# A hybrid decoder step: GpSimd's arithmetic moved to VectorE, adaLN's scale in two halves, and the first tokens' norm applied behind the first products

## The chip, the cores and the metric

The kernel runs on one core of one Trainium2 chip. The metric is the device time of one execution in microseconds, as the median of several runs; the profile is of one further execution. The core's engines are TensorE (PE, with its weight loads PEld), VectorE (DVE), ScalarE (ACT), GpSimd (POOL) and SyncE (SP). Each has its own instruction queue and takes it in order; DMAs are issued from queues of SP, ACT and POOL.

## The reference

One inference step of a decoder layer over 1,024 new prompt tokens and 8 sequences of 4 sampled tokens (1,056 tokens, width 1,024). Only what the change touches is shown:

```python
mod = jax.nn.silu(c) @ w_ada + b_ada
sh1, sc1, g1, sh2, sc2, g2 = jnp.split(mod, 6, axis=-1)
h = _rmsnorm(x, rms1_g) * (1 + sc1[:, None, :]) + sh1[:, None, :]
z = h @ w_in + b_in            # q, k, v, forget, glu_a, glu_b, gate_a, gate_b
o = attend(q, k, v, logf)
y_a = o.reshape(B, L, ATT_WIDTH) @ w_pa
y_b = _depthwise_causal_conv(u_pad, dw_w, dw_b)      # u = glu_a * sigmoid(glu_b)
y_b = jax.nn.silu(_layernorm(y_b, ln_g, ln_b)) @ w_pb + b_pb
m = gate_a * y_a + gate_b * y_b
x = x + g1[:, None, :] * (m @ w_o)
```

A SwiGLU feed-forward part with the same kind of norm and modulation follows.

## The kernel before, in words

**Precision and products.** Activations and weights are split in a high part and a remainder (`wh`, `wl` for weights, `ah`, `al` for activations). A product is three matmuls per 128 rows of the inner dimension: `wh` by `ah` (L327), `wh` by `al` (L328), `wl` by `ah` (L329). ACT rounds a weight to `wh` (L315), and the engine that `split_w` is given subtracts to get `wl` (L318). A weight tile is 128x1024 (eight inner blocks) or, for the two output projections of the branches, 128x512.

**Tokens.** They come in three chunks, c0 and c1 of 384 tokens and c2 of 288 (256 of the prompt and the 32 sampled ones). Tiles hold features on partitions.

**Start.** `ada(i)` makes one sixth of the adaLN vector: eight loads `wa` of 512 KB, 32 matmuls against the conditioning vectors (L161), a copy by ACT (L165), two transposes (L170) and an addition (L173). `ada(1)` is the scale; with it `gains` makes `gP` (L180) and `gS` (L181). For c0 and c1 `rstd_x` sums squares and gives the reciprocal root, `normalise` (L283) multiplies it onto x in place, and `split_scaled` splits x·gP into `ah` (L291, ACT) and `al` (L292, DVE). The products of four weights with c0 and c1 (the Q and K columns of two pairs of heads) are taken from these while the shift, `ada(0)`, is still being loaded. They are copied to `early` tiles by ACT (L412). c2 is split with the shift already in (`modulate`, L249 to L273). When the shift is there, `split_shifted` splits c0 and c1 once more with the shift (L300 DVE, L301 ACT, L302 half on POOL, half on DVE), and the shift's own share of the early products is added as a bias, from two extra columns of c2.

**After the start.** The remaining Q and K pairs and V follow (to about 219 us). The stage from 219 to 428 us computes the convolution branch's inputs (`glu`), the depthwise convolution on DVE (120 instructions at L528, 128x1024 each), the gates and the decoding attention (`decode_group`, L692 to L748). Attention over the prompt takes 428 to 690 us, with the layer norm of the convolution (`conv_ln`, sums at L775 to L777 and L231 on POOL) and the other parts of `ada` between. From 690 to 795 us `branch` computes the two output projections, with an addition by POOL at L968 for the attention branch. From 795 us on the output product and the feed-forward part run, where POOL does no arithmetic.

**What sets the order.** A framework schedules the instructions of each engine ahead of time. `in_order` pins an instruction to program order among pinned ones, and `tc.high_priority()` moves a block ahead. Each engine then takes its list in order and waits at each entry for what it needs. Weights come through three raw buffers `wr` and two pairs `wh`, `wl`, so the split of one weight can begin when the product before the last has ended.

```python
def w_in_tile(i, eng=dve, q=sp):
    return split_ahead(w_in[i], KD, eng, q=q)
        wb = w_in_tile(12 + ct, pool, pool)
```

The second `pool` in such calls is the queue that the load of the weight is issued from.

Of the kernel before, what the change touches and what calls it, by code (L numbers as in the profile page):

```python
# [9 lines left out]
F32 = mybir.dt.float32  # L10
# [3 lines left out]
OP = mybir.AluOpType  # L14
# [72 lines left out]
def hybrid_step(ctx, tc, xT, cT, vec, bvf, con, stT, ptab, ptabr, kcT, vc, lfc, w_ada, w_in, w_vfa, w_vfb,  # L87
# [4 lines left out]
    def mkpool(**kw):  # L92
        return tc.alloc_tile_pool(reuse_waits="tile", **kw)
# [47 lines left out]

    def load_x(c):
        o, n = CH[c]
        t = x0.tile([P, KD, n], F32, name=f"x{c}")
        in_order(sp.dma_start(t, xT[:, KD * o:KD * (o + n)].rearrange("p (k n) -> p k n", k=KD)))
        xt.append(t)


    act.activation(cTt, cTt, AF.Silu)
    wap = mkpool(name="wap", bufs=1, side="right")  # L150

    def ada(i, pl, tag, bufs, psum):

        ps = psum()
        for k in range(KD):
            w = pl.tile([P, KD, P], F32, name="wa", tag=tag, bufs=bufs).rearrange("p a b -> p (a b)")
            d = sp.dma_start(w, w_ada[k * P:(k + 1) * P, i * 1024:(i + 1) * 1024])
            if i < 2:
# [4 lines left out]
        with tc.high_priority() if i < 2 else nullcontext():  # L163
            s = ev(wp, "gev", 4)
            d = act.copy(s[:, :256], ps[:, :256])  # L165
            if i == 1:
                in_order(d)
# [7 lines left out]
            if i == 1:  # L175
                gains(0, V_RMS1, 8)

    def gains(i, vcol, sc):
        g = V[:, vcol:vcol + KD]
        dve.scalar_tensor_tensor(gP[:, i, :], mod[:, sc:sc + KD, 0], 1.0, g, op0=OP.add, op1=OP.mult)  # L180
        dve.scalar_tensor_tensor(gS[:, i, :, :], mod[:, sc:sc + KD, 1:9], 1.0,  # L181
                                 g.unsqueeze(2).broadcast_to([P, KD, DB]), op0=OP.add, op1=OP.mult)
# [39 lines left out]

    def sumsq(tiles, n, eng=dve):
        s = sm.tile([P, 400], F32, name="ssum", tag="ssum", bufs=2)
        for i, t in enumerate(tiles):
            if i == 0:
                act.activation(s[:, :n], t, AF.Square)
            else:
                q = ev(sm, "sq", 2, (P, 400))
                act.activation(q[:, :n], t, AF.Square)  # L230
                eng.tensor_tensor(s[:, :n], s[:, :n], q[:, :n], OP.add)  # L231
        return s
# [61 lines left out]

    def split_shifted(c, eng):
        x = xt[c]
        ah, al = A[c] = act_tiles(c)
        for k in range(KD):
            t = ev(w0p, "mt", 3)
            dve.tensor_scalar(t, x[:, k, :], gP[:, 0, k:k + 1], mod[:, k, 0:1], OP.mult, OP.add)  # L300
            act.copy(ah[:, k, :], t)  # L301
            (eng if k % 2 else dve).tensor_tensor(al[:, k, :], t, ah[:, k, :].bitcast(F32), OP.subtract)  # L302
# [42 lines left out]


    w0p = mkpool(name="w0p", bufs=1)
    load_x(0)
    in_order(sp.dma_start(C[:, :C_MASK], con[:, :C_MASK]))
    in_order(sp.dma_start(V, vec))  # L350
# [11 lines left out]
    first_w(1, pool)  # L362
    first_w(2, pool, w0p, ("wh0", "wl0"))
    first_w(3, pool, w0p, ("wh0", "wl0"))
    normalise(1, rstd_x(1))
    split_scaled(1, dve)
    load_x(2)
    ada(0, wap, "wa", 5, ps_tr)
    wap.release()
# [125 lines left out]
    def glu(ct):  # L495
# [3 lines left out]
        sp.dma_start(us[:, :, 0:KL], stT[ct].rearrange("p (b i) -> p b i", b=DB))  # L499
        wb = w_in_tile(12 + ct, pool, pool)  # L500
        sg = []
        for c in range(3):
# [4 lines left out]
            sg.append(t)  # L507
        wa = w_in_tile(8 + ct, pool, pool)
        for c in range(3):
# [243 lines left out]
    glu(1)  # L753
    gate(15, pool, pool)
    glu(2)
    gate(14, pool, pool)
    gate(13, pool, pool)
    glu(3)
    for i in (12, 11, 10):
        gate(i, pool, pool)  # L760

# [5 lines left out]
    def conv_ln(c):  # L767
# [15 lines left out]
        pr = rstd(sumsq(xc, n, pool), n, CW)  # L783
        for ct in range(4):
# [189 lines left out]
    gate(7, pool, sp)  # L974
    ap.release()
# [433 lines left out]
```

## Time and profile before

| what | value |
| --- | --- |
| median of 3 runs | 1636.25 us (1630.43 to 1641.71) |
| profiled execution, own time | 1629.88 us |
| its span from first to last instruction | 1628.1 us |
| mean granted clock of TensorE | 0.992 of full speed |
| PE busy | 1564.1 us (96%) |
| DVE busy | 1048.5 us (64%) |
| ACT busy | 697.3 us (43%) |
| POOL busy | 178.2 us (11%), 147 instructions |

Own time and span differ by 1.8 us that lie around the span. In rows of groups and of the timeline, the first number is the start (timeline) or the line, `x8` counts instructions joined in a row, and what stands in brackets behind a row is the idle time ahead of it on its engine with what ended it. The clock is given as a share of 2.4 GHz, so that 0.5 is 1.2 GHz.

### The profile page before, as it was taken

To read this page: it belongs to the slowest core of one execution; us is meant where nothing else is said; L and a number is where in the kernel's file an instruction comes from. 1 tells how busy PE (TensorE), PEld (TensorE's weight loads), DVE (VectorE), ACT (ScalarE), POOL (GpSimd) and SP (SyncE) were. 2 spreads that over 40 slices of the span, in tenths; PEclk is the share of its full clock that TensorE was granted. 3 is DMA by queue.
4 is the path that set the end of the run, shared out by engine and by line. 5 is a ranking of instruction groups with operands and counts; after the bars stand their busy time and mean duration, and the time that the engine had idled before them with its cause. 6 is when DMAs were issued, how large, how long until landed. Compare 5 with 4: busy or idle time off the path is not lost.

```text
span 1628.1 us, 29682 instructions
## 1 busy us (share of the span) xinstructions
PE 1564.1 (96%) x11280; PEld 1475.9 (91%) x11280; DVE 1048.5 (64%) x2161; ACT 697.3 (43%) x1398; POOL 178.2 (11%) x147
## 2 busy tenths in 40 slices
PE   6999999999999989999999999999999999999997
PEld 4899978788977878999899989999999999999997
DVE  6942469999888867244559995555555596324644
ACT  4552112121376766434426663333333375224342
POOL 2121022342220101024200000000000000000000
PEclk9999999999999999999999999999999999999998
DMA  9195476777787774453554322222222257424552
GB/s 358 65 305 177 144 218 184 249 243 201 213 235 242 210 211 153 143 175 114 185 175 150 120 88 92 80 79 80 79 79 80 79 184 242 129 82 142 187 178 81
DMA packets 141424, 261.86 MB, mean 161 GB/s; under 512 B 24634, under 2 KB 81594, under 8 KB 140642
## 3 DMA queue, kind: packets, MB, share of 16 engines
q1 hardware_dynamic: 102802, 209.37, 41.0%
q10 hardware_dynamic: 36384, 43.01, 7.6%
q0 software_dynamic: 2096, 7.60, 1.5%
q8 instruction: 88, 1.44, 0.4%
q14 instruction: 54, 0.44, 0.1%
HBM read 206.44 MB, written 53.48 MB: 160 GB/s over the span
## 4 chain that ended last, share of the span: by engine, by line
PE 72%; DVE 12%; DMA 7%; ACT 3%; issue 3%; POOL 2%; SPq 1%; ACTq 0%; DVEq 0%; POOLq 0%
PE mm L1177 25%; PE mm L1278 16%; PE mm L329 7%; PE mm L328 7%; PE mm L327 7%; DVE acc L528 4%; DMA wa<-w_ada 2%; DMA gev<-gD 2%; POOL wl L318 1%; PE ptr L874 1%; PE mm L561 1%; PE mm L560 1%; PE mm L562 1%; DMA sq<-hD 1%; PE ppv L887 1%
## 5 line engine op out<-in xcount | busy, mean ns | idle before, releaser
L327 PE MATMUL mm<-ah,wh 128*128 128x384 f32 (+2 forms) x768 | 252.9, 330 | 8.8 <-ACT gev L384 4.0
L1278 PE MATMUL mm<-f,wo 128*128 128x352 f32 x1584 | 256.8, 323 | 0.0
L1278 PEld LDWEIGHTS mm<-f,wo 128*128 128x128 f32 x1584 | 254.8, 188 | 0.0
L329 PE MATMUL mm<-ah,wl 128*128 128x384 f32 (+2 forms) x768 | 251.5, 329 | 2.2 <-POOL wl L318 2.2
L328 PE MATMUL mm<-al,wh 128*128 128x384 f32 (+2 forms) x768 | 252.6, 329 | 0.0
L1177 PE MATMUL mm<-c,wc 128*128 128x264 f32 x1776 | 235.3, 285 | 1.5 <-ACT gev L1182 0.9
L1177 PE MATMUL mm<-b,wc 128*128 128x264 f32 x1680 | 228.1, 286 | 3.7 <-DVE wc L1135 1.5
L1177 PEld LDWEIGHTS mm<-c,wc 128*128 128x128 f32 x1776 | 224.1, 188 | 2.4 <-ACT gev L1182 1.3
L1177 PEld LDWEIGHTS mm<-b,wc 128*128 128x128 f32 x1680 | 214.7, 189 | 5.1 <-ACT wc L1134 2.0
L528 DVE SCALAR_TENSOR_TENSOR acc<-u,vec,acc 128x1024 f32<-128x1024 f32 x120 | 173.9, 1471 | 1.2
L327 PEld LDWEIGHTS mm<-ah,wh 128*128 128x128 f32 x768 | 145.9, 190 | 18.3 <-issue 5.9
L328 PEld LDWEIGHTS mm<-al,wh 128*128 128x128 f32 x768 | 146.3, 190 | 11.2 <-issue 10.4
L318 POOL TENSOR_TENSOR wl<-wr,wh 128x1024 fp32r<-128x1024 f32 (+1 forms) x44 | 111.8, 2545 | 396.0 <-ACT wh L315 340.9
L1229 DVE TENSOR_TENSOR wo<-wr,wo 128x512 fp32r<-128x512 f32 x108 | 69.7, 646 | 129.5 <-ACT wo L1228 128.9
L329 PEld LDWEIGHTS mm<-ah,wl 128*128 128x128 f32 x768 | 146.1, 190 | 6.3 <-POOL wl L318 3.1
L1134 ACT CAST wc<-wr 128x512 fp32r<-128x512 f32 x144 | 88.6, 621 | 141.4 <-PE mm L1177 132.4
L1228 ACT CAST wo<-wr 128x512 fp32r<-128x512 f32 x108 | 63.2, 585 | 150.6 <-PE mm L1278 143.3
L1135 DVE TENSOR_TENSOR wc<-wr,wc 128x512 fp32r<-128x512 f32 x144 | 98.5, 689 | 36.0 <-ACT wc L1134 35.0
L315 ACT CAST wh<-wr 128x1024 fp32r<-128x1024 f32 (+1 forms) x64 | 59.7, 939 | 93.1 <-PE mm L328 56.6
L192 POOL MEMSET rv<- 128x5 f32 x7 | 0.7, 103 | 746.2 <-DVE rt L210 746.2
L329 PE MATMUL mm<-b,wl 128*128 128x264 f32 x256 | 72.3, 286 | 2.2 <-DVE wl L318 2.2
L327 PE MATMUL mm<-b,wh 128*128 128x264 f32 x256 | 72.9, 285 | 1.3 <-ACT wh L315 1.3
(294 smaller groups left out, 2735.5 us busy)
## 6 DMA issues: line engine op xcount, KB each, us to landing
wr<-w_fi SPq DMA_DIRECT2D x52, 512.0 KB
wa<-w_ada SPq DMA_DIRECT2D x48, 512.0 KB
wr<-w_fo SPq DMA_DIRECT2D x36, 512.0 KB
kt<-kcT SPq DMA_DIRECT2D x64, 256.0 KB
vt<-vc SPq DMA_DIRECT2D x64, 256.0 KB
hD<-h ACTq DMA_DIRECT2D x44, 264.0 KB
wr<-w_in SPq DMA_DIRECT2D x18, 512.0 KB
wr<-w_o SPq DMA_DIRECT2D x16, 512.0 KB
```

What stands on the lines that cost most here:

```text
L315: d = act.copy(wh[:, r, :], raw[:, r, :])
L318: eng.tensor_tensor(wl[:, r, :], raw[:, r, :], wh[:, r, :].bitcast(F32), OP.subtract)
L327: pe.matmul(ps[:, :n], wh[:, k, :], xh, start=(k == 0), stop=False)
L328: pe.matmul(ps[:, :n], wh[:, k, :], xl, start=False, stop=False)
L329: pe.matmul(ps[:, :n], wl[:, k, :], xh, start=False, stop=(k == nk - 1))
L528: dve.scalar_tensor_tensor(a[:, :NP], u[:, j:j + NP], wv[:, j:j + 1], a[:, :NP], op0=OP.mult, op1=OP.add)
L1134: act.copy(w[:, 0, :n], raw)
L1135: dve.tensor_tensor(w[:, 1, :n], raw, w[:, 0, :n].bitcast(F32), OP.subtract)
L1177: pe.matmul(ps[:, :HS], w[i][:, r, k * P:(k + 1) * P], x[s][:, k, :], start=(new and k == 0 and j == 0), stop=(k == 3 and j == 2), skip_gr ...
L1228: act.copy(x[:, 0, :], raw)
L1229: dve.tensor_tensor(x[:, 1, :], raw, x[:, 0, :].bitcast(F32), OP.subtract)
L1278: pe.matmul(ps[e][:, :n], w[r][:, k * P:(k + 1) * P], f[x], start=(k0 + k + i == 0), stop=(k0 + k == HT - 1 and i == 2))
```

## The change

GpSimd's arithmetic goes to VectorE: all 44 subtractions `wl` that it did (30 of 128x1024, 14 of 128x512), the 28 additions at L968, the sums of `conv_ln`, and its eight subtractions in `split_shifted`. It keeps memsets, some small copies and the DMA issues. The scale is made by `ada_half`, four loads of 512 KB for each half of its columns, and x of c0 is loaded in two halves, so that the first products can be taken from inner blocks 0 to 3. `normalise` is gone: c0 and c1 are split as they come, and the reciprocal root, copied to a tile `rx` in SBUF, is multiplied onto the first products by DVE where ACT copied them. The second split of c0 and c1 is done by `modulate`. The first four weights are split in two halves each. The loads of the shift have four buffers where they had five.

```diff
-    def load_x(c):
+    def load_x(c, k0=0, k1=KD):
...
+    def ada_half(i, half, pl):
+
+        ps = ps_tr()
+        o = i * 1024 + half * 512
+        for k in range(0, KD, 2):
+            w = pl.tile([P, 2, 512], F32, name="wa", tag="wa", bufs=4)
+            in_order(sp.dma_start(w, w_ada[k * P:(k + 2) * P, o:o + 512].rearrange("(k p) n -> p k n", p=P)))
+            for j in range(2):
+                for g in range(4):
+                    pe.matmul(ps[32 * g:32 * g + 32, :P], cTt[:, k + j, :], w[:, j, g * P:(g + 1) * P],
+                              start=(k + j == 0), stop=(k + j == KD - 1))
...
+            dve.scalar_tensor_tensor(gP[:, 0, k], mod[:, r, 0], 1.0, g, op0=OP.add, op1=OP.mult)
...
     def rstd_x(c):
         n = CH[c][1]
-        return rstd(sumsq([xt[c][:, k, :] for k in range(KD)], n), n, D)
-
-    def normalise(c, pr):
-
-        for k in range(KD):
-            x = xt[c][:, k, :]
-            dve.tensor_tensor(x, x, pr[:, :CH[c][1]], OP.mult)
+        r = w0p.tile([P, n], F32, name=f"rx{c}")
+        act.copy(r, rstd(sumsq([xt[c][:, k, :] for k in range(KD)], n), n, D)[:, :n])
+        return r
...
-    def split_shifted(c, eng):
...
-        step = 8 if pinned else nk
+        step = 4 if pinned else nk
...
-    load_x(0)
     in_order(sp.dma_start(C[:, :C_MASK], con[:, :C_MASK]))
     in_order(sp.dma_start(V, vec))
-    pr = rstd_x(0)
-    ada(1, wap, "wa", 5, ps_tr)
-    normalise(0, pr)
...
-    first_w(0, pool)
+    ada_half(1, 0, wap)
+    first_w(0, dve)
+    load_x(0, 0, 4)
+    first_w(1, dve)
+    first_w(2, dve, w0p, ("wh0", "wl0"))
+    load_x(0, 4)
+    ada_half(1, 1, wap)
     split_scaled(0, dve)
+    first_w(3, dve, w0p, ("wh0", "wl0"))
     load_x(1)
...
-    normalise(1, rstd_x(1))
     split_scaled(1, dve)
+    norms = [rstd_x(0), rstd_x(1)]
+    gains(0, V_RMS1, 8)
     load_x(2)
-    ada(0, wap, "wa", 5, ps_tr)
+    ada(0, wap, "wa", 4, ps_tr)
...
-            act.copy(early[c, i], ps[:, :384])
+            dve.tensor_tensor(early[c, i], ps[:, :384], norms[c], OP.mult)
...
-        split_shifted(c, pool)
+        modulate(c, xt[c], norms[c], 0, 0, w0p, dve)
...
-        wb = w_in_tile(12 + ct, pool, pool)
+        wb = w_in_tile(12 + ct, dve, pool)
...
-        pool.tensor_tensor(s[:, :n], xc[0], xc[1], OP.add)
+        dve.tensor_tensor(s[:, :n], xc[0], xc[1], OP.add)
...
-            w = split_ahead(w_p[j], 4, pool)
+            w = split_ahead(w_p[j], 4)
...
-        (pool if j < KD - 1 else dve).tensor_tensor(zg, zg, X(j)[:, o:o + HS], OP.add)
+        dve.tensor_tensor(zg, zg, X(j)[:, o:o + HS], OP.add)
```

Lines of the changed kernel are numbered otherwise: the products L327, L328, L329 are L336, L337, L338 there, `wl` L318 is L327, the convolution L528 is L539, `al` of x·gP L292 is L310.

SP's queue at the start, from its first entry, in the kernel before (`x` with 3072 elements is a chunk of 384 tokens):

```order
L138 DMA cT<-cT 128x256
L145 DMA x_89<-xT 128x3072
L349 DMA con<-con 128x256
L350 DMA vec<-vec 128x248
L157 DMA wa<-w_ada 128x1024 x8
L309 DMA wr<-w_in 128x1024
L145 DMA x_232<-xT 128x3072
```

The same place in the changed kernel (1536 elements are a half of c0):

```order
L138 DMA cT<-cT 128x256
L363 DMA con<-con 128x256
L364 DMA vec<-vec 128x248
L159 DMA wa<-w_ada 128x2x512 x4
L318 DMA wr<-w_in 128x1024
L146 DMA x_146<-xT 128x1536
L318 DMA wr<-w_in 128x1024 x2
L146 DMA x_146<-xT 128x1536
L159 DMA wa<-w_ada 128x2x512 x4
L318 DMA wr<-w_in 128x1024
L146 DMA x_238<-xT 128x3072
```

x of c0 moved from ahead of the scale's eight loads to behind its first four, in two halves, with three weights around them.

PE's list at the start, in the changed kernel, from the end of the 36 first products with c0 (`pst<-con,ssum` sums the squares, `ptr<-con,gev` is the transpose of a half of the scale; before, all 32 matmuls of `ada` and both transposes stood ahead of the first product):

```order
L337 MATMUL mm<-al_213,wh 128x384
L338 MATMUL mm<-ah_212,wl 128x384
L162 MATMUL ptr<-wa,cT 32x128 x24
L220 MATMUL pst<-con,ssum 128x1 x3
L162 MATMUL ptr<-wa,cT 32x128 x8
L168 MATMUL ptr<-con,gev 128x128
L336 MATMUL mm<-ah_212,wh 128x384 x3
L337 MATMUL mm<-al_213,wh 128x384
L338 MATMUL mm<-ah_212,wl 128x384
```

The second half's 32 matmuls now stand between products with c0: 36 of the 96 ahead of them, 60 behind.

DVE's list in the stage of the convolution, at its third channel block, before (`acc` is the convolution, `dt` the decoding attention):

```order
L528 SCALAR_TENSOR_TENSOR acc<-u,vec,acc 128x1024 x2
L701 SCALAR_TENSOR_TENSOR dt<-ppv,cr,ct 128x4
L528 SCALAR_TENSOR_TENSOR acc<-u,vec,acc 128x1024 x13
L700 TENSOR_SCALAR dt<-pss,cr 128x512
L528 SCALAR_TENSOR_TENSOR acc<-u,vec,acc 128x1024 x2
```

And in the changed kernel:

```order
L539 SCALAR_TENSOR_TENSOR acc<-u,vec,acc 128x1024
L712 SCALAR_TENSOR_TENSOR dt<-ppv,cr,ct 128x4
L539 SCALAR_TENSOR_TENSOR acc<-u,vec,acc 128x1024 x9
L327 TENSOR_TENSOR wl<-wr,wh 128x1024
L539 SCALAR_TENSOR_TENSOR acc<-u,vec,acc 128x1024 x8
L711 TENSOR_SCALAR dt<-pss,cr 128x512
L539 SCALAR_TENSOR_TENSOR acc<-u,vec,acc 128x1024 x2
L711 TENSOR_SCALAR dt<-pss,cr 128x512
L327 TENSOR_TENSOR wl<-wr,wh 128x1024
L539 SCALAR_TENSOR_TENSOR acc<-u,vec,acc 128x1024 x2
```

A `wl` that had POOL's list to itself now stands behind up to nine steps of the convolution, and convolution steps stand behind it.

## Rows read from the trace of the kernel before

**Rows 1.** Page, part 1: busy time, share of the span and instructions of each engine.
```profile
PE 1564.1 (96%) x11280; PEld 1475.9 (91%) x11280; DVE 1048.5 (64%) x2161; ACT 697.3 (43%) x1398; POOL 178.2 (11%) x147
```

**Rows 2.** Busy time by stage: length, engines, then PEclk, DMA share, GB/s.
```profile
0.00:26.80 26.80, 12.03 (x78) 5.04 (x78) 11.69 (x35) 7.60 (x14) 2.55 (x5) 1.00 0.89 347
...
219.00:428.00 209.00, 202.81 (x1344) 169.03 (x1337) 206.46 (x225) 40.60 (x64) 60.90 (x24) 0.99 0.76 229
428.00:690.00 262.00, 248.65 (x1772) 216.65 (x1771) 183.36 (x576) 166.75 (x334) 34.36 (x29) 0.99 0.65 195
690.00:795.00 105.00, 101.08 (x716) 99.41 (x716) 49.80 (x92) 46.60 (x103) 43.32 (x43) 1.00 0.48 149
```

**Rows 3.** Timeline, 0 to 32.5 us: start, length, engine, line, operation.
```profile
10.64 2.28 PE L161 MATMUL ptr<-wa,cT 128*32 128x256 f32 x16 [10.64 <-DMA wa<-w_ada]
...
21.24 1.08 PE L161 MATMUL ptr<-wa,cT 128*32 128x256 f32 x8
21.34 3.81 DVE L283 TENSOR_TENSOR x<-x,pst 128x384 f32<-128x384 f32 x8 [2.66 <-PE pst L220]
...
26.86 0.69 PE L327 MATMUL mm<-ah,wh 128*128 128x384 f32 x1 [3.36 <-ACT ah L291]
...
28.32 0.52 PE L327 MATMUL mm<-ah,wh 128*128 128x384 f32 x1
...
28.64 0.52 PE L328 MATMUL mm<-al,wh 128*128 128x384 f32 x1
...
31.99 0.34 PE L327 MATMUL mm<-ah,wh 128*128 128x384 f32 x1
...
32.17 0.33 PE L328 MATMUL mm<-al,wh 128*128 128x384 f32 x1
```

**Rows 4.** Timeline of PE, then of DVE, 54 to 74 us.
```profile
55.54 0.97 PE L327 MATMUL mm<-ah,wh 128*128 128x384 f32 x4
...
73.75 0.44 PE L327 MATMUL mm<-ah,wh 128*128 128x290 f32 x2
...
61.09 0.21 DVE L173 TENSOR_TENSOR mod<-ptr,vec 128x72 f32<-128x72 f32 x1
...
69.69 0.42 DVE L269 TENSOR_TENSOR al<-ms,ah 128x256 fp32r<-128x256 f32 x1
```

**Rows 5.** Groups of POOL, then DVE by form: count, busy, mean ns, idle before.
```profile
L318 POOL TENSOR_TENSOR wl<-wr,wh 128x1024 fp32r<-128x1024 f32 (+1 forms) x44 | 111.8, 2545 | 396.0 <-ACT wh L315 340.9 <-PE mm L329 16.6 <-PE pss L818 15.1
...
L528 DVE SCALAR_TENSOR_TENSOR acc<-u,vec,acc 128x1024 f32<-128x1024 f32 x120 | 173.9, 1471 | 1.2
...
L318 DVE TENSOR_TENSOR wl<-wr,wh 128x1024 fp32r<-128x1024 f32 x20 | 24.4, 1231 | 6.8 <-ACT wh L315 6.6
...
L967 DVE TENSOR_TENSOR gev<-mm,gev 128x264 f32<-128x264 f32 x32 | 13.6, 426 | 15.5 <-ACT gev L956 13.7 <-PE mm L329 1.7
L283 DVE TENSOR_TENSOR x<-x,pst 128x384 f32<-128x384 f32 x16 | 7.6, 542 | 2.7 <-PE pst L220 2.7
```

**Rows 6.** Timeline of DVE and POOL, 320 to 428 us, and of PE at 339.
```profile
320.93 15.63 DVE L528 SCALAR_TENSOR_TENSOR acc<-u,vec,acc 128x1024 f32<-128x1024 f32 x13
399.55 28.47 DVE L528 SCALAR_TENSOR_TENSOR acc<-u,vec,acc 128x1024 f32<-128x1024 f32 x17
...
322.14 16.62 POOL L318 TENSOR_TENSOR wl<-wr,wh 128x1024 fp32r<-128x1024 f32 x1 [16.69 <-ACT wh L315]
...
400.14 2.96 POOL L318 TENSOR_TENSOR wl<-wr,wh 128x1024 fp32r<-128x1024 f32 x1 [11.27 <-ACT wh L315]
424.31 2.64 POOL L318 TENSOR_TENSOR wl<-wr,wh 128x1024 fp32r<-128x1024 f32 x1 [9.95 <-ACT wh L315]
...
338.81 0.57 PE L329 MATMUL mm<-ah,wl 128*128 128x384 f32 x1 [2.22 <-POOL wl L318]
```

**Rows 7.** What PE waited for, whole span: us in total, times, longest.
```profile
PE mm L329 <- POOL wl L318: 5.0, 5, 2.2
```

**Rows 8.** Busy time after that wait: PEclk is the third number from the end.
```profile
339.00:342.30 3.30, 3.30 (x11) 3.30 (x11) 3.27 (x2) 0.00 (x0) 3.01 (x3) 0.50 0.86 299
```

More of the change, by code (lines that the diff above doesn't have):

```diff
@@ L140, in hybrid_step @@
     in_order = tc.keep_in_program_order
-    def load_x(c):
+    def load_x(c, k0=0, k1=KD):
         o, n = CH[c]
-        t = x0.tile([P, KD, n], F32, name=f"x{c}")
-        in_order(sp.dma_start(t, xT[:, KD * o:KD * (o + n)].rearrange("p (k n) -> p k n", k=KD)))
-        xt.append(t)
+        if k0 == 0:
+            xt.append(x0.tile([P, KD, n], F32, name=f"x{c}"))
+        in_order(sp.dma_start(xt[c][:, k0:k1, :],
+                              xT[:, KD * o + k0 * n:KD * o + k1 * n].rearrange("p (k n) -> p k n", n=n)))
     act.activation(cTt, cTt, AF.Silu)
     wap = mkpool(name="wap", bufs=1, side="right")
+    def ada_half(i, half, pl):
[8 more added lines that the diff above has]
+                              start=(k + j == 0), stop=(k + j == KD - 1))
+        with tc.high_priority():
+            s = ev(wp, "gev", 4)
+            act.copy(s[:, :P], ps[:, :P])
+            pt = ps_tr()
+            pe.transpose(pt[:, :P], s[:, :P], ident)
+            src = pt[:, :P].rearrange("p (g r) -> p g r", g=4)[:, :, 0:9]
+            r = slice(i * 8 + half * 4, i * 8 + half * 4 + 4)
+            b = V[:, V_ADA + r.start:V_ADA + r.stop]
+            dve.tensor_tensor(mod[:, r, :], src, b.unsqueeze(2).broadcast_to([P, 4, 9]), OP.add)
+            k = slice(half * 4, half * 4 + 4)
+            g = V[:, V_RMS1 + half * 4:V_RMS1 + half * 4 + 4]
+            dve.scalar_tensor_tensor(gP[:, 0, k], mod[:, r, 0], 1.0, g, op0=OP.add, op1=OP.mult)
     def ada(i, pl, tag, bufs, psum):
@@ L157, in ada @@
             d = sp.dma_start(w, w_ada[k * P:(k + 1) * P, i * 1024:(i + 1) * 1024])
-            if i < 2:
+            if i == 0:
                 in_order(d)
@@ L162, in ada @@
                           start=(k == 0), stop=(k == KD - 1))
-        with tc.high_priority() if i < 2 else nullcontext():
+        with tc.high_priority() if i == 0 else nullcontext():
             s = ev(wp, "gev", 4)
-            d = act.copy(s[:, :256], ps[:, :256])
-            if i == 1:
-                in_order(d)
+            act.copy(s[:, :256], ps[:, :256])
             pt = psum()
@@ L174, in ada @@
                               src, b.unsqueeze(3).broadcast_to([P, 4, 2, 9]), OP.add)
-            if i == 1:
-                gains(0, V_RMS1, 8)
     def gains(i, vcol, sc):
         g = V[:, vcol:vcol + KD]
-        dve.scalar_tensor_tensor(gP[:, i, :], mod[:, sc:sc + KD, 0], 1.0, g, op0=OP.add, op1=OP.mult)
+        if i:
+            dve.scalar_tensor_tensor(gP[:, i, :], mod[:, sc:sc + KD, 0], 1.0, g, op0=OP.add, op1=OP.mult)
         dve.scalar_tensor_tensor(gS[:, i, :, :], mod[:, sc:sc + KD, 1:9], 1.0,
@@ L221, in rstd, with sumsq @@
         return prs if n > 512 else prs[0]
-    def sumsq(tiles, n, eng=dve):
+    def sumsq(tiles, n):
         s = sm.tile([P, 400], F32, name="ssum", tag="ssum", bufs=2)
@@ L230, in sumsq @@
                 act.activation(q[:, :n], t, AF.Square)
-                eng.tensor_tensor(s[:, :n], s[:, :n], q[:, :n], OP.add)
+                dve.tensor_tensor(s[:, :n], s[:, :n], q[:, :n], OP.add)
         return s
@@ L293, in split_scaled @@
                                      op0=OP.mult, op1=OP.subtract)
-    def split_shifted(c, eng):
[L296 to L302, printed above, removed]
     def split_w(src, nk, eng=dve, pl=wp, tags=("wh", "wl"), bufs=2, q=sp, pinned=False):
@@ L357, in first_w @@
         first.append(split_w(w_in[(0, 4, 1, 5)[i]], KD, eng, *where, pinned=True))
-    first_w(0, pool)
+    in_order(sp.dma_start(C[:, :C_MASK], con[:, :C_MASK]))
+    in_order(sp.dma_start(V, vec))
+    ada_half(1, 0, wap)
[5 more added lines that the diff above has]
+    ada_half(1, 1, wap)
     split_scaled(0, dve)
+    first_w(3, dve, w0p, ("wh0", "wl0"))
     load_x(1)
-    first_w(1, pool)
-    first_w(2, pool, w0p, ("wh0", "wl0"))
-    first_w(3, pool, w0p, ("wh0", "wl0"))
-    normalise(1, rstd_x(1))
     split_scaled(1, dve)
+    norms = [rstd_x(0), rstd_x(1)]
+    gains(0, V_RMS1, 8)
     load_x(2)
-    ada(0, wap, "wa", 5, ps_tr)
+    ada(0, wap, "wa", 4, ps_tr)
     wap.release()
@@ L507, in glu @@
             sg.append(t)
-        wa = w_in_tile(8 + ct, pool, pool)
+        wa = w_in_tile(8 + ct, dve, pool)
         for c in range(3):
@@ L753, in hybrid_step @@
     glu(1)
-    gate(15, pool, pool)
+    gate(15, dve, pool)
     glu(2)
-    gate(14, pool, pool)
-    gate(13, pool, pool)
+    gate(14, dve, pool)
+    gate(13, dve, pool)
     glu(3)
     for i in (12, 11, 10):
-        gate(i, pool, pool)
+        gate(i, dve, pool)
     cvp.release()
@@ L774, in conv_ln @@
         s = sm.tile([P, 400], F32, name="lnsum", tag="ssum", bufs=2)
-        pool.tensor_tensor(s[:, :n], xc[0], xc[1], OP.add)
+        dve.tensor_tensor(s[:, :n], xc[0], xc[1], OP.add)
         for ct in (2, 3):
-            pool.tensor_tensor(s[:, :n], s[:, :n], xc[ct], OP.add)
+            dve.tensor_tensor(s[:, :n], s[:, :n], xc[ct], OP.add)
         dve.tensor_scalar(s[:, :n], s[:, :n], 1.0 / CW, None, OP.mult)
@@ L782, in conv_ln @@
             dve.tensor_tensor(xc[ct], xc[ct], pm[:, :n], OP.subtract)
-        pr = rstd(sumsq(xc, n, pool), n, CW)
+        pr = rstd(sumsq(xc, n), n, CW)
         for ct in range(4):
@@ L915, in hybrid_step @@
     for i in (9, 8, 6, 5, 4, 3, 2, 1, 0):
-        gate(i, pool, sp)
+        gate(i, dve, sp)
         if 3 <= i < 7:
@@ L972, in hybrid_step @@
     branch(1, cvD, w_pb, CW3, out_b)
-    gate(7, pool, sp)
+    gate(7, dve, sp)
     ap.release()
```

2 lines of the change are left out of this document (removed).

## The prediction

> **What bounds the kernel now.** First the page's busy shares: PE is busy 96% of the span, DVE 64%, ACT 43%, POOL 11% [rows 1]. So a gain can only come from stretches in which PE stands still, runs at the lower clock, or does the wrong thing, and the second view is the busy time by stage. In the first 26.8 us PE is busy 12.0 us, but with the adaLN matmuls alone: the first product of tokens and weights starts at 26.86 [rows 2, 3], and the DMAs move 347 GB/s the whole time. That stage is bound by loading. From 219 to 428 us PE is busy 202.8 of 209.0 and DVE 206.5, so two engines are near full. Attention leaves PE 13.4 us of 262, the branches 3.9 of 105 [rows 2]. Behind 795 us nothing of the change is at work. Third, the timeline of the start, for the order in which the loads and the chain behind them end [rows 3, 4]; fourth, the groups of POOL and DVE for the price of an operation on either [rows 5]; fifth, the timeline where both run at once [rows 6]; last, PE's waits, of which POOL's `wl` makes 5.0 us in five times [rows 7].
>
> **The start.** Before, the bytes ahead of the first `wa` are x of c0 (1,536 KB) and that load (512 KB), and it is there at 10.64 [rows 3]. After, the four loads of the first half are the same 2,048 KB, so all of them are there at about 10.6. Behind them come w0 (512 KB, 1.5 us at 347 GB/s) and half of c0 (768 KB, 2.3 us): 14.4. Splitting one block takes about half a microsecond (the DVE subtraction of such a block 0.54 by the nearest row [rows 5]), so the first product starts at about 15, not 26.86. It has 36 products to do (inner blocks 0 to 3 of three weights). At the lower clock they step 0.32 us (28.32 to 28.64), at the higher 0.18 (31.99 to 32.17) [rows 3], and before, the higher one was there 5.1 us behind the first product: 16 slow and 20 fast ones make 8.7 us, all slow ones 11.5. They end between 23.7 and 26.5.
>
> The second half's loads come behind w1, w2, the other half of c0 and themselves: 512 + 512 + 768 + 2,048 KB, 11.3 us on 14.4, so 25.7. Before, the last adaLN matmuls began at 21.24 and the first product at 26.86, 5.6 us later, of which the normalisation held DVE from 21.34 to 25.15 [rows 3]. It is gone, so the chain lies between 1.7 (what came behind it) and 5.6 us. I take 2.6, as its matmuls and transpose are half as many. The second batch then starts at 28.3. Sixty products at 0.175 us are 10.5, and up to 2.3 more where the clock has fallen in between: c1 starts at 39 to 41, where it was 55.54 [rows 4], 15 us ahead.
>
> Most of that lead is not kept, as c2 needs the shift. Its loads lie behind 512 KB (w3), 1,536 (c1), 1,152 (c2), two weights and another, and they are 4,096 themselves: 8.8 MB from 25.7 at 347 GB/s make about 51, with the last matmuls and the addition 52.5 to 54. Before, that addition was at 61.09, and the last of c2's splits began at 69.69 and ended at 70.1, 9.0 us later; c2's products started at 73.75 behind those of c1 [rows 4]. Now DVE has up to four evacuations of some 0.54 us more in that time (ACT copied them before), 11 us in all: c2 can start at 64 to 65. The products with c1 (18.2 us, and some 3 us of adaLN matmuls and sums among them) end at 60 to 62, so the splits of c2 are last. Gain 73.75 - 65 = 8.7. Over the whole start DVE loses 16 normalising steps (0.54 us each, 8.7 us) and gains eight subtractions of POOL's (4.3) and the first four weights' `wl` (4 x 1.23): a draw. But afterwards it has the shifted splits of c0 and c1 alone, some 20 us of work, and can give back a few microseconds. I take -8.5, with bounds -12 (c1's end decides) and -2.
>
> **What the clock may cost there.** Between the two batches PE stands for two to four microseconds. In this trace a stand of 2.22 us at 338.81 is followed by 3.3 us at a granted clock of 0.50 [rows 6, 8], which costs 1.7 us. The Trainium skill (TensorE: Matmul & The Clock Gate, HAM oscillation — how this bites in real kernels) speaks against such a split: products that come in batches with a wait for a load between them start each batch at the lower clock. The trace agrees in the row at 339. By the rule the start would be cold twice, some 2 us more than if it stayed warm; that is inside the bounds above.
>
> **The convolution's stage.** Fourteen `wl` of 128x1024 go from POOL to DVE there. On DVE one takes 1.23 us [rows 5], 17.2 us in all, behind an engine that is busy 206.5 of 209. But POOL's `wl` hold DVE up: thirteen steps of the convolution in 15.63 us are 1.20 us each, and during them POOL's `wl`, at 322.14, takes 16.62 us; seventeen steps take 28.47 where 17 x 1.20 is 20.4, and the three POOL rows in that time (first and last shown) are 2.96, about 2.6 and 2.64, in sum the 8.1 that are over [rows 6]. So one engine stands for the whole operation of the other. Over all 120 steps the mean is 1.47 against 1.20, 32 us [rows 5]. DVE's load in the stage thus falls by 32 and rises by 17: it has more room than before, about 15 us. PE has not: of its 6.2 us of idle time the one wait for `wl` is 2.22 [rows 6], and the lower clock behind it cost 1.7. These two go: -3.9. What can come in their place is a `wl` that stands behind up to nine steps of the convolution in DVE's list (nine are 10.8 us), or a step that waits behind a `wl` for ACT. A product tile over all three chunks is 72 matmuls, about 12.6 us, and with two buffers that is the time from the buffer's release to the next need. So a `wl` up to 10 us late costs nothing, and bounds are -6.2 (no idle time left) and +15 (a microsecond lost for each of 14).
>
> **The branches.** POOL's `wl` of 128x512 made four of the five waits, 5.0 - 2.2 = 2.8 us [rows 7]. DVE takes 0.65 us each for half of 1.23, and 28 additions of 0.43 by the nearest row (L967, the same shape [rows 5]): some 20 us more on an engine busy 49.8 of 105 [rows 2]. Some waits of DVE remain in place of POOL's. I take -2, bounds -3.9 and +3.
>
> **Attention.** Eighteen sums of `conv_ln` (0.54 us by the row of the same shape, 10 us) and about nine `wl` (11 us) are added to DVE, busy 183 of 262 [rows 2, 5], less what POOL held it up there. PE's 13.4 us of idle time can shrink or grow. I take 0, bounds -8 and +6.
>
> Sum: -8.5 - 3.9 - 2 + 0 = -14.4 on the profiled execution's own 1629.88, so 1615.5. The median of the runs shown is 6.4 above it; on that scale 1636.25 - 14.4 = 1621.9, and I say 1621.
>
> **Rivals.** *More than that* (A): DVE was what PE waited for in more places than the trace names, because POOL held it. Then the idle times of three stages shrink further: conv -6, attention -8, branches -3, start -8.5, in sum -25, so 1611. For it speaks that DVE is full in the conv stage and that 32 us of stretch go; against it that PE is full there too. The Trainium skill (SBUF — State Buffer, Who interferes with whom) has the same lock: a DVE instruction with two inputs in SBUF and a reading GpSimd one share a port pair, and one blocks wholly. By it no step of DVE is stretched any more once POOL's arithmetic is gone, and A's 1611 is the time. The 16.62 us row agrees with the lock, and no row shows what PE makes of it.
>
> *The start is given back* (B): c2 or the shifted splits wait for DVE, which now has four evacuations, all `wl` and all eight odd subtractions, or for the shift's loads with four buffers, whose second four need PE to reach the matmuls among c1's products. Then the start brings 2 or nothing, the rest -2 to -4: about -4, so 1632. For it speaks that the 9 us from the addition to c2's last split were DVE's list, not a load [rows 4]; against it that the loads begin 10 us ahead.
>
> *Slower* (C): in the conv stage the scheduled DVE list does not fit the real times. A `wl` behind eight or nine steps comes later than its 10 us of cover, and the step behind a `wl` waits for ACT. With 14 weights late by 2.2 us each (the length of the one wait there is) that is 31 us, less 8.5 and 2 elsewhere: +20, so 1656. It outweighs the gains from about three quarters of a microsecond a weight on. For it speaks that the two engines have 3 and 6 us of room in 209; against it the 15 us that DVE gains.
>
> **How the numbers follow.** The forecast has 0.45, A 0.25, B 0.20, C 0.10. One per cent (16.4 us, about what a measurement of this kernel tells from no change) parts them at 1619.9. Of the forecast, whose own spread is some 6 us on either side, two fifths lie below that: 0.18; of A nearly all, 0.23; together 0.41. C, of which about 0.04 lies under 1652.6, leaves 0.06 for slower, and 0.53 stay within. The range takes the forecast, A and B with their bounds and leaves out C and the far end of A: 1603 to 1638.
>
> **What would show it.** Right: a first product at about 15 us, a pause and a second batch at 28, c2's products (290 columns) at 64 to 65; no `wl` on POOL; convolution steps of 1.20 us throughout, and no wait of PE for `wl` of 2 us in the conv stage. A shows as idle time of PE under 8 us in attention. B shows as PE waiting for the `al` of c2 or of the shifted splits past 70 us. C shows as waits of PE for DVE's `wl` many times in 219 to 428. The forecast is wrong if c2's products start past 70 us, or if PE's busy time itself changes by more than 5 us, which no step here expects.

## The result, and the profile after

The changed kernel takes 1642.55 us (median of 8 runs, 1637.99 to 1647.12), the kernel before 1632.22 in the same session (8 runs): a ratio of 1.0071, 95% interval 1.0053 to 1.0088. It is slower, where 1621 was forecast (0.991 of before's 1636.25). The profiled execution took 1640.72 us with a span of 1639.0.

What the change removes is gone, as its page shows (part 1):

```profile
span 1639.0 us, 29737 instructions
...
PE 1568.8 (96%) x11344; PEld 1485.7 (91%) x11344; DVE 1052.2 (64%) x2257; ACT 698.9 (43%) x1397; POOL 19.8 (1%) x49
```

POOL went from 178.2 to 19.8 us, and DVE, which took its work over, from 1048.5 to 1052.2: what it gained in work it lost in stretch. The groups of DVE (by form) say the same, beside [rows 5]:

```profile
L539 DVE SCALAR_TENSOR_TENSOR acc<-u,vec,acc 128x1024 f32<-128x1024 f32 x120 | 149.9, 1280 | 0.7
...
L327 DVE TENSOR_TENSOR wl<-wr,wh 128x1024 fp32r<-128x1024 f32 x44 | 53.6, 1223 | 22.6 <-ACT wh L324 22.3
```

The convolution's steps fell from 173.9 to 149.9 us. Yet the whole is longer. The busy time by stage, of stretches that answer to [rows 2] (the second from 219 to the first score, the third to attention's last product, the fourth to the first product of the output weights):

```profile
0.00:26.80 26.80, 16.27 (x172) 12.68 (x172) 11.32 (x29) 11.13 (x22) 0.20 (x4) 1.00 0.95 360
219.00:418.00 199.00, 193.85 (x1283) 159.35 (x1284) 179.04 (x228) 39.35 (x62) 4.49 (x10) 0.98 0.73 217
418.00:692.90 274.90, 251.63 (x1779) 221.28 (x1777) 200.85 (x610) 164.95 (x332) 0.31 (x3) 0.97 0.67 193
...
692.90:803.90 111.00, 108.08 (x747) 107.00 (x746) 64.81 (x132) 50.26 (x106) 0.00 (x0) 0.97 0.52 159
```

Attention, from the first score to the last product with V, had been

```profile
410.50:672.00 261.50, 249.06 (x1775) 217.75 (x1773) 195.67 (x581) 161.59 (x327) 38.32 (x30) 0.99 0.68 201
```

in the kernel before. The start of landmarks of PE in both traces, in us:

| landmark | before | after | difference |
| --- | --- | --- | --- |
| first product of tokens and weights | 26.86 | 14.73 | -12.1 |
| c2's first product (290 columns) | 73.75 | 68.09 | -5.7 |
| c2's last product | 86.57 | 85.03 | -1.5 |
| V's first product | 139.25 | 139.92 | +0.7 |
| first score of attention | 410.49 | 418.02 | +7.5 |
| last product with V of attention | 671.98 | 692.85 | +20.9 |
| first product of the output weights | 790.34 | 803.91 | +13.6 |
| end of the span | 1628.1 | 1639.0 | +10.9 |

"Gate products" are from here on the products with the weights `w_in` of Q, K, glu and all gates but gate 7, 2,232 in all. PE's list in the changed kernel has 1,625 of them ahead of the first score where it had 1,584, and 607 between there and the last product with V where it had 603. So most of the +6.8 us of the conv stage are work done earlier (41 products), and the branches have 45 fewer left to do. What is lost is attention's: nearly the same matmuls, 274.8 us for 261.5. The start's 12 us are gone by 139 us. Some 2.7 us come back behind 804, where no run looks.

The loss can be read in the clock as well. The mean granted clock is 0.982 in the changed kernel's eight runs (0.979 to 0.985), and 0.989 in the 101 runs of the kernel before beside the experiments (0.984 to 0.993). By an estimate from these numbers, 0.007 of 1640 us are 11 to 12 us at full speed, about the whole loss. In the traces the lower clock mostly follows a stand of PE, so it tells how the loss is paid and not what made PE stand.

### The profile page after: what moved, and what is told of

It is laid out like the page before. It is cut to its first block, busy times and chain, and to the rows that moved or that the text cites. A ratio compares the mean times of both kernels' runs of the same rounds, so it can differ in the third digit from the quotient of the medians.

```text
span 1639.0 us, 29737 instructions
## 1 busy us (share of the span) xinstructions
PE 1568.8 (96%) x11344; PEld 1485.7 (91%) x11344; DVE 1052.2 (64%) x2257; ACT 698.9 (43%) x1397; POOL 19.8 (1%) x49
## 4 chain that ended last, share of the span: by engine, by line
PE 76%; DMA 10%; DVE 8%; ACT 3%; issue 2%; SPq 2%; ACTq 0%; DVEq 0%; POOLq 0%
PE mm L1188 25%; PE mm L1289 16%; PE mm L336 8%; PE mm L337 8%; PE mm L338 8%; PE ptr L885 1%; DMA wa<-w_ada 1%; DVE acc L539 1%; DMA gev<-gD 1%; PE mm L572 1%; PE mm L571 1%; PE mm L573 1%; PE ppv L898 1%; PE pss L826 1%; PE pss L829 1%
## 5 line engine op out<-in xcount | busy, mean ns | idle before, releaser
L336 PE MATMUL mm<-ah,wh 128*128 128x384 f32 (+2 forms) x768 | 254.8, 333 | 10.5 <-ACT gev L395 6.0
L337 PE MATMUL mm<-al,wh 128*128 128x384 f32 (+2 forms) x768 | 253.8, 331 | 1.1 <-DVE al L291 1.1
L338 PE MATMUL mm<-ah,wl 128*128 128x384 f32 (+2 forms) x768 | 254.3, 331 | 0.0
L336 PEld LDWEIGHTS mm<-ah,wh 128*128 128x128 f32 x768 | 147.4, 192 | 23.2 <-issue 10.0
L337 PEld LDWEIGHTS mm<-al,wh 128*128 128x128 f32 x768 | 147.9, 193 | 8.6 <-issue 6.2
L338 PEld LDWEIGHTS mm<-ah,wl 128*128 128x128 f32 x768 | 148.0, 193 | 6.6 <-issue 5.8
L539 DVE SCALAR_TENSOR_TENSOR acc<-u,vec,acc 128x1024 f32<-128x1024 f32 x120 | 149.9, 1280 | 0.7
L327 DVE TENSOR_TENSOR wl<-wr,wh 128x1024 fp32r<-128x1024 f32 (+1 forms) x68 | 69.7, 1033 | 33.4 <-ACT wh L324 33.0
L336 PE MATMUL mm<-b,wh 128*128 128x264 f32 x256 | 72.7, 285 | 0.5 <-ACT wh L324 0.5
L338 PE MATMUL mm<-b,wl 128*128 128x264 f32 x256 | 72.2, 285 | 0.9 <-DVE wl L327 0.9
L337 PE MATMUL mm<-b,wh 128*128 128x264 f32 x256 | 72.4, 283 | 0.0
```

The costliest lines, as they stand in the source:

```text
L327: eng.tensor_tensor(wl[:, r, :], raw[:, r, :], wh[:, r, :].bitcast(F32), OP.subtract)
L336: pe.matmul(ps[:, :n], wh[:, k, :], xh, start=(k == 0), stop=False)
L337: pe.matmul(ps[:, :n], wh[:, k, :], xl, start=False, stop=False)
L338: pe.matmul(ps[:, :n], wl[:, k, :], xh, start=False, stop=(k == nk - 1))
L539: dve.scalar_tensor_tensor(a[:, :NP], u[:, j:j + NP], wv[:, j:j + 1], a[:, :NP], op0=OP.mult, op1=OP.add)
```

## Experiments

All ratios are to the kernel before, run beside it. In each, what is not named stays as in the kernel it starts from.

**The start alone.** The changed kernel with POOL as before behind the start (15 places of the kind shown; no line of the start is touched):

```diff
-        wb = w_in_tile(12 + ct, dve, pool)
+        wb = w_in_tile(12 + ct, pool, pool)
...
-        dve.tensor_tensor(s[:, :n], xc[0], xc[1], OP.add)
+        pool.tensor_tensor(s[:, :n], xc[0], xc[1], OP.add)
```

> The changed start alone; everything behind it (glu, gates, layer norm of the convolution, branches) splits and adds on POOL as before. Theory (the start's lead is spent by 140 us, and the 11 us are lost in attention): c2's products start near 68 us, V near 140, attention takes the 261 us it took before, and the time is within 2 us of before (ratio 0.999 to 1.001). Rival (the changed start does harm that comes out later): the time stays about 10 us over before (1.006).

Measured: 1.0008 (0.9993 to 1.0024); c2 at 67.6, V at 138.5, attention 263.4. The start brings nothing, and does no harm.

**The later part alone.** The kernel before with the reverse of these edits.

> The start of before, and all of POOL's later arithmetic on DVE. Theory: the loss of the whole change is here, +9 to +13 us (ratio 1.006 to 1.008), with attention 12 to 15 us longer than before's 261. Rival (the start does the harm): within 2 us of before.

Measured: 1.0067 (1.0043 to 1.0091); attention 277.2 us. The whole loss is in the later part, and most of it in attention.

**The convolution's stage on POOL again.** The changed kernel with glu and the gates 15 to 10 split on POOL (`gate(15, pool, pool)` and so on).

> The changed kernel, but the weights of glu and of the gates 15 to 10 are split on POOL again. Theory (the loss is made where DVE's list in attention is longer): little comes back, 1.004 to 1.008. Rival (the convolution's stage runs ahead with gate products, and attention lacks them): attention has 45 products more to fill with, and the time falls to within 3 us of before.

Measured: 1.0015 (0.9995 to 1.0035), attention 276.2 us, with 648 gate products in it, 45 more than before. 9 us came back (1.0071 to 1.0015), nearer to the rival, but with these products discounted (some 7 us) attention is still longer than before's 261.5. The layer norm's sums are on DVE here, as in the changed kernel, and most of the loss is gone all the same. With the lists everything shifts; this run alone settled nothing.

**Attention's POOL work on POOL again.** The sums of the convolution's layer norm and the nine gates' weights.

> The changed kernel, but the sums of the convolution's layer norm and the weights of the nine gates in attention are done on POOL again. Theory: attention is back at some 262 us and the time within 3 us of before. Rival (PE's list has no products left for attention's end, 2,220 of 2,232 being placed ahead of the last score): it stays 6 to 12 us over before.

Measured: 1.0017 (0.9998 to 1.0035), attention 268.9. The time is the theory's, attention's length is not (262 were expected), and there are two edits in one.

**One of the two: the layer norm's sums on POOL,** all weights on DVE:

```diff
-        dve.tensor_tensor(s[:, :n], xc[0], xc[1], OP.add)
+        pool.tensor_tensor(s[:, :n], xc[0], xc[1], OP.add)
         for ct in (2, 3):
-            dve.tensor_tensor(s[:, :n], s[:, :n], xc[ct], OP.add)
+            pool.tensor_tensor(s[:, :n], s[:, :n], xc[ct], OP.add)
...
-        pr = rstd(sumsq(xc, n), n, CW)
+        pr = rstd(sumsq(xc, n, pool), n, CW)
```

> The changed kernel with the sums of the convolution's layer norm alone back on POOL; all weights stay on DVE. PE's list has 2,205 of 2,232 gate products ahead of the last score. If the sums are what holds attention up, most of the 5.4 us that the fourth run got back are here (1.002 to 1.003); if the weights are, 1.005 to 1.007.

Measured: 1.0010 (0.9998 to 1.0022), under the range expected. Without these 18 additions of 0.55 us on DVE the changed kernel is a draw; all the rest of the change costs, in sum, nothing that can be measured. That holds of the whole, not of attention: in this run's profile attention takes 269.4 us, 5.4 under the changed kernel's and still 7.9 over before's, with 17.2 us at the lower clock (17.1 in the changed kernel). Gains outside attention make up for most of that.

**The same, the other way round.** The kernel before with that one edit, 18 additions moved to DVE:

> The kernel before with one edit: the layer norm's sums (18 additions) on DVE; its start, all weight splits and the branches as before. PE's list is nearly that of before (2,068 gate products ahead of the last score, 2,072 before). Theory (DVE waits at the sums for the loads with the softmax behind it): the one edit brings most of the whole change's loss, 1.004 to 1.007, with DVE waits of 5 to 10 us for xc. Rival (the wait hurts only together with the earlier gate products of the changed kernel): 1.000 to 1.003.

Measured: 1.0082 (1.0058 to 1.0106), 1643.94 us, as slow as the whole change and a little over the range expected; attention takes 276.0 us. DVE's waits there, in 400 to 700 us:

```profile
DVE xc L790 <- ACT sq L789: 5.6, 3, 3.0
...
DVE lnsum L775 <- DMA xc<-acD: 3.7, 1, 3.7
...
DVE lnsum L777 <- DMA xc<-acD: 0.8, 1, 0.8
```

The wait for the loads was 4.5 us, under the 5 to 10 expected, while the loss was 13; another 5.6 are waits in the layer norm's last step. Two of PE's waits in attention, and a stretch behind the second (the third number from the end is the clock):

```profile
PE pss L815 <- DVE mx L820: 4.7, 4, 2.6
...
PE ptr L874 <- DVE px L831: 2.2, 1, 2.2
```

```profile
523.50:533.50 10.00, 6.90 (x32) 5.05 (x30) 5.13 (x16) 5.68 (x11) 0.00 (x0) 0.50 0.99 340
```

PE stood 2.2 us until 434, behind the first chunk's sums, and 2.65 until 523, behind a last step that had waited 3.0 us for ACT. The clock was then at 0.50 for 3.4 and for 10.2 us. The stands and half of these stretches make some 11.6 of the 13 us, an estimate. But DVE does that last step in the kernel before too, so the edit shifted it in time; why it stood there is not shown.

**What the sums cost DVE.** The view of the tile `lnsum` in the changed kernel, DVE's idle time ahead of its instructions (us, times):

```profile
its engine sat idle before it (us, times) until:
  DMA xc<-acD: 10.2, 4
```

Its timeline at the first and the third sum, 438 and 539 us:

```profile
438.06 0.22 DVE L836 SCALAR_TENSOR_TENSOR st<-mx,Cq 128x1 f32<-128x1 f32 x1
443.11 0.56 DVE L786 TENSOR_TENSOR lnsum<-xc 128x384 f32<-128x384 f32 x1 [4.83 <-DMA xc<-acD]
...
535.14 0.69 DVE L842 TENSOR_SCALAR px<-px,st 128x896 f32<-128x896 f32 x1
539.14 0.46 DVE L786 TENSOR_TENSOR lnsum<-xc 128x288 f32<-128x288 f32 x1 [3.31 <-DMA xc<-acD]
539.52 0.75 DVE L831 CUSTOM_DVE_ANT_0 px<-pss,ck,mx 128x512 f32<-128x512 f32 x1
```

and PE behind it, which needs a score buffer that DVE has yet to read:

```profile
536.32 0.39 PE L829 MATMUL pss<-kl,q 128*128 128x384 f32 x1
540.33 0.79 PE L826 MATMUL pss<-k,q 128*128 128x512 f32 x1 [3.62 <-DVE mx L831]
```

At the third sum DVE stands for an input that is still on its way from DRAM (the convolution's result is stored and loaded again), the softmax stands behind the sum, and PE behind the softmax; the granted clock then falls to one half for 3.4 us at 540. At the first sum PE had gate products for the whole 4.8 us and did not stand; at the second it stood 1.35 us. So of DVE's 10.2 us some 5.0 reach PE, 6.7 with what the clock takes behind the third (an estimate from these rows), and that is not the whole of attention's loss. In the kernel before the sums stood in POOL's list, with nothing of the softmax behind them. The row was there to be read:

```profile
L775 POOL TENSOR_TENSOR lnsum<-xc 128x384 f32<-128x384 f32 (+1 forms) x3 | 2.8, 940 | 60.3 <-DMA xc<-acD 34.4 <-PE mm L161 25.9
```

**Work or wait?** The sums stay on DVE, as many and as long, but the loads are issued first and the rest of the layer norm, its additions included, stands six units of attention later; the sum is put into a row buffer `py`, which the scheduler can hand out only then:

```diff
-    def conv_ln(c):
+    def ln_load(c):
...
+        return xc
+
+    def conv_ln(c, xc):
+        o, n = CH[c]
-        s = sm.tile([P, 400], F32, name="lnsum", tag="ssum", bufs=2)
+        s = ptile(0)
...
         if n in (0, 8, 16):
-            conv_ln(n // 8)
+            xc = ln_load(n // 8)
+        if n in (6, 14, 22):
+            conv_ln(n // 8, xc)
```

> The changed kernel with the layer norm's sums still on DVE and as many, but the sum goes into one of the softmax's small row buffers and stands six units of attention behind the loads of its input, so that DVE never comes to it before the loads have landed (in the changed kernel DVE stood 10.2 us there, with the softmax queued behind). Theory (the standing in DVE's queue is the price, not the work of the sums): DVE's wait for the loads of xc is gone, attention is 6 to 10 us shorter than the changed kernel's 275, and the time is 1.000 to 1.003 of before. Rival (the 10 us of added work on DVE are the price): it stays at 1.005 to 1.008.

Measured: 0.9995 (0.9980 to 1.0009), a little better than the theory's range. Attention:

```profile
414.20:678.20 264.00, 249.23 (x1778) 217.60 (x1776) 201.54 (x610) 161.53 (x330) 0.80 (x3) 0.99 0.69 201
```

No wait for the loads of xc is among DVE's waits any more. DVE is busy 201.5 us there, 200.9 in the changed kernel: the work is the same, and 10.9 us of attention are gone. The price was the place in the list, not the work. The other steps of the layer norm moved with the sums, and the lists shifted around them; what of the 10.9 us is each one's is not separated.

**Products held for attention's end.** PE's list of the changed kernel has all 2,232 gate products ahead of the last score (2,072 before), and nothing to fill the last softmax. From 673.8 to 692.9 us:

```profile
673.80:692.90 19.10, 12.12 (x67) 10.79 (x65) 8.20 (x20) 13.98 (x28) 0.00 (x0) 0.73 0.18 48
```

The weights of gates 1 and 0 are loaded into row buffers, which come free late (`raw` is handed on to `split_w`):

```diff
-        gate(i, dve, sp)
+        gate(i, dve, sp, raw=ptile(2).rearrange("p (k n) -> p k n", n=P) if i < 2 else None)
```

> The changed kernel, but the weights of the last two gates (1 and 0, 144 products, 24 us of PE) are loaded into two of the softmax's row buffers, which come free only when the last head's rows are transposed. PE's list then has 2,088 of its 2,232 gate products ahead of the last score, where the changed kernel has all 2,232 and the kernel before 2,072. DVE's work is the changed kernel's. Theory (attention's end is bare because its filling was used up): attention and branches together lose 8 to 11 us less, the time is within 3 us of before (0.999 to 1.002). Rival (DVE's added work makes attention's chain late, wherever the products stand): the time stays 8 to 12 us over before (1.005 to 1.007).

Measured: 1.0027 (1.0014 to 1.0040), a little outside the theory's range and far from the rival's. Holding the products back gave some 7 us. The bare end does not come from the sums: the lists are made ahead of time, and 2,205 products stand ahead of the last score with the sums on POOL, 2,068 with the sums alone on DVE. Nor does it decide by itself: the run with the sums behind their loads has 2,222 there, and is faster. Here, as in the run with the convolution's stage on POOL (1.0015), the sums stand on DVE in their old place, DVE waits 12.0 us (5.8 in that run) for their loads, and most of the loss is gone. Why the sums cost so little in these two lists, and 13 us in that of before, is not shown.

**V's loads.** The changed start alone, with the loads of V's weights issued from POOL's queue:

```diff
-        sp.dma_start(raw, src.rearrange("p (k n) -> p k n", k=KD))
+        pool.dma_start(raw, src.rearrange("p (k n) -> p k n", k=KD))
```

> The changed start with POOL's later arithmetic as before (as the first run), and V's two weight loads issued from POOL's queue, not behind the K and Q stores on SP's. Theory (the start's lead is lost because ACT's list has V's weights ahead of an evacuation, and they are loaded late): PE's wait of 4 us near 119 us goes, V starts 3 to 5 us before 138.5, and the time is 2 to 5 us under the first run's (0.998 to 0.999 of before). Rival (something else holds V at 139, the stores through DRAM or POOL's own queue): no change, 1.000 to 1.002.

Measured: 0.9973 (0.9961 to 0.9985), 0.35% under the start alone and better than expected, V at 137.6 in its profile (the lead is 0.9 us there, less than expected; PE's wait for the evacuations was 4.3 us where it was 6.4). The load `w_vfa`, issued at 105.7 here, stood in the run of the start alone behind these stores in SP's queue:

```profile
102.31 6.96 SPq L407 DMA_DIRECT2D qkD<-qkl  x2
...
109.86 0.48 SPq L556 DMA_DIRECT2D vr<-w_vfa  x1
```

**The branches on DVE,** on top of the changed start (`split_ahead(w_p[j], 4)`, the additions and gate 7):

> As the first run, but the branches' weights and additions and gate 7 on DVE, as in the changed kernel. Theory (the branches alone gain from it): PE's waits for POOL's weights there (2.8 us) go, and the time is 2 to 4 us under the first run's (0.998 to 0.9995 of before). Rival (DVE's list gets the same waits): within 1 us of the first run.

Measured: 0.9976 (0.9965 to 0.9987), 0.32% under the start alone. PE's waits for POOL's weights in the branches, 3.7 us in the start-alone run, are gone. This part of the change is a gain.

**Both of these together.** By the order in which they were run, the two above are runs 6 and 7.

> The changed start, V's loads on POOL's queue and the branches' arithmetic on DVE; glu, gates and layer norm sums on POOL as before. If the gains of the two runs (6 and 7) add up on the first one's 1.0008, 0.9935 to 0.995. If the start's gain is lost again later, 0.997 to 0.998.

Measured: 0.9962 (0.9948 to 0.9976), 1624.40 us. V starts at 134.1, 5 us ahead, but attention takes 266.1; the gains add up in part. It is the lowest time of the kernels tried, though its interval overlaps those of both.

**Both mendings on the changed kernel.** The ninth run is the one with the sums behind their loads, the sixth that of V's loads.

> The changed kernel with both mendings: the sums stand behind their loads (as in the ninth run) and V's loads are issued from POOL's queue (as in the sixth). No arithmetic on POOL. If both add up on 1.0071: 1.0071 - 0.0076 - 0.0035 = 0.996 of before, 6 us less. If V's loads bring nothing here (c2's stage gave the lead back already): 0.9995.

Measured: 0.9976 (0.9960 to 0.9993), between the two. With no arithmetic on POOL at all and both mendings the change is a small gain.

## Why the prediction was wrong

**The step that failed: attention, "I take 0, bounds -8 and +6".** It priced the 18 sums as work (10 us on an engine with room) and did not ask what each of them waits for. Measured: attention +13.4 us. Moving the sums alone costs as much as the whole change (1.0082), and without them the change is a draw (1.0010), though attention alone is then still 7.9 us longer. On POOL the sums held up nothing of the softmax while they waited for a load; on DVE the softmax stood behind them. The prediction did ask what is queued behind a wait for the weights in the convolution's stage, where it did not matter. PE's waits in attention in the changed kernel, the largest three:

```profile
PE mm L186 <- DMA wa<-w_ada: 9.5, 6, 3.4
PE pss L826 <- DVE mx L831: 5.6, 3, 3.6
PE ppv L897 <- ACT pth L887: 4.3, 2, 3.8
```

The same in the kernel before:

```profile
PE mm L161 <- DMA wa<-w_ada: 5.6, 5, 2.5
...
PE pss L815 <- DVE mx L820: 0.5, 1, 0.5
```

The second row is where the sums reach PE. The loads of `ada`, and the end without products (3.8 us of the third row), grew beside it. How the 13 us divide between the standing itself (10.2 us on DVE in the changed kernel, 4.5 where the one edit was made), the lower clock behind it, the loads and the bare end stays open; the run that moved the sums took 10.9 us away at once.

**The start, -8.5.** First product at 14.73 for 15, the 36 products done at 23.1 for 23.7, second batch at 27.71 for 28.3, as worked out; 3.4 us from 28.3 on were at the lower clock. The shift was late: 59.06 for 52.5 to 54. PE and DVE in the changed kernel:

```profile
54.20 0.64 PE L186 MATMUL ptr<-wa,cT 128*32 128x256 f32 x8
...
58.65 0.38 PE L193 MATMUL ptr<-con,gev 128*128 128x128 f32 x2
...
59.06 0.23 DVE L196 TENSOR_TENSOR mod<-ptr,vec 128x72 f32<-128x72 f32 x1 [1.52 <-PE ptr L193]
```

The last matmuls of the shift were done at 54.8, and products with c1 stood ahead of the two transposes for 3.8 us: PE's list, which the prediction had at hand, was not priced there. DVE's list behind it took 10.9 us to c2's last split, where 11 were worked out. The products with c1 were mis-sized as well: they began at 40.66, for 39 to 41, but ended at 66.6 and not at 60 to 62, with PE busy without a break, and 8.3 us of adaLN matmuls, sums and transposes among them, where the prediction had some 3. So c2 began at 68.09, only 1.5 us behind them, and then waited for its own splits:

```profile
68.09 0.80 PE L336 MATMUL mm<-ah,wh 128*128 128x290 f32 x4 [1.48 <-ACT ah L290]
69.98 0.61 PE L337 MATMUL mm<-al,wh 128*128 128x290 f32 x1 [1.08 <-DVE al L291]
```

From the second of these waits on the clock was at one half for 6.8 us of the profiled execution, and c2's 96 products took 17.1 us for 13.0:

```profile
69.30:76.00 6.70, 6.02 (x25) 6.02 (x26) 6.70 (x14) 3.74 (x7) 0.00 (x0) 0.50 0.00 0
```

The Trainium skill (TensorE: Matmul & The Clock Gate, HAM oscillation — how this bites in real kernels) describes batches that start at the lower clock after a wait for a load. The trace agrees as to the fall between the two batches, where the prediction put it (3.4 us from 28.3 on), though PE had adaLN matmuls there and stood for 1.14 us only. At c2 the waits were for splits and shorter, 1.48 and 1.08 us, and the clock fell there too. The start-alone run had no such fall there (14.4 us), and its lead was gone at V all the same. What takes the rest is a bound that the prediction did not look for. ACT and PE at 120 us:

```profile
120.48 2.18 ACT L562 CAST vh<-vr 128x512 fp32r<-128x512 f32 x4 [6.98 <-DMA vr<-w_vfa]
122.56 0.40 ACT L404 CAST qkh<-gev 128x256 fp32r<-128x256 f32 x1
122.87 0.57 ACT L395 ACTIVATE gev<-mm,bqk 128x384 f32<-128x384 f32 x1
...
123.50 0.40 PE L336 MATMUL mm<-ah,wh 128*128 128x288 f32 x1 [4.07 <-ACT gev L395]
```

ACT stands at V's weights, whose load sits in SP's queue behind the stores of Q and K; the evacuation that frees PE's next accumulator is behind it. A start that is ahead meets this and gives its lead back. In the eight profiles with the changed start and V's loads on SP's queue, c2's last product starts at 81.5 to 82.2 in five and at 84.9 to 85.2 in three, and V at 137.8 to 139.9 in all. With the loads on POOL's queue the time from the one to the other is 51.9 to 53.1 us in three profiles, where it is 54.3 to 56.8 in those eight and 52.7 before. Rival B (the start is given back, 0.20 of the chance) was right in the start's result; of its places c2's wait for `al` is there (1.08 us), but the larger part lies at V. With V's loads on another queue 0.35% came back.

**The convolution's stage, -3.9.** The mechanism was right: no wait of PE for a `wl` there, and steps of DVE near the undisturbed 1.20 us (1.25 in the mean). The gain did not come: net of the 41 products done earlier (about 6.6 us at 0.16 us a product) the stage is as long as before (+0.2 us). The standing moved to the decoding keys. PE's waits, 219 to 418 us:

```profile
PE pss L703 <- DMA kt<-kcT: 4.3, 2, 2.6
PE ppv L744 <- DMA vt<-vc: 0.9, 2, 0.7
```

where they were 3.1 and 2.2 (for `wl`). Rival C, that weights come late there, did not happen.

**The branches, -2.** Right in kind and under-sized by the run on top of the start: -5 us (1.0008 to 0.9976). POOL's `wl` were 16 of 128x512 and 28 of 128x1024 in the trace of before, not 14 and 30. In the changed kernel's own profile the gain does not show: 118.4 us became 111.1 with 45 products fewer (some 7 us), and 6.8 us behind attention's bare end were at the lower clock.

**Attention's idle time as a gain (rival A).** Its sign was under 8 us of idle time of PE in attention; there were 23.3. DVE has lost its stretch there as well, and with the sums in a better place 0.9995 is all that it brings.

**What the prediction watched.** Its two signs of being wrong did not show: c2's products started at 68.09 (past 70 was the sign), and PE's busy time changed by 4.7 us (more than 5). They watched the start and the amount of work; what failed was a wait. That the result lies within one per cent, which had 0.53 of the chance, is no merit of the sum, which was to be 0.9% faster. Slower had 0.06, for the convolution's stage, where the loss was not.

## What to carry to other kernels

Before an instruction is moved to a busier engine, read the idle column of its row as well as its length: what it waits for today at no price is waited for by everything behind it tomorrow. An engine with nothing to do is a good place for an instruction that waits. A lead at the start is worth what the next fixed point leaves of it, here a load in a queue behind stores; look for that point before pricing the lead.

## What was not expected of the hardware

A DVE instruction and a POOL instruction that read two tensors each excluded one another for the whole operation in the trace of before ([rows 6]); taking all of POOL's arithmetic away gave DVE back 24 us of the convolution's steps and no time of the kernel's. And short stands of PE cost more than their length: 3.62 us at 540 were followed by 3.4 us at the lower clock. Attention had 17.1 us of it in the changed kernel's profile, 23.9 in that of the one edit, 6.8 before and 6.8 with the sums behind their loads; but also 17.2 with the sums on POOL, so it is not the sums' doing alone.
